# A hybrid decoder layer on one Trainium2 core: squares summed in small tiles, memory's norm later, quarters prepared over six units, pooling ahead of the local attention, constants loaded later

## The chip, the core and the metric

The kernel runs on one core of a Trainium2 chip. The core has a matrix engine (TensorE, PE in the profile), a vector engine (VectorE, DVE), a scalar engine (ScalarE, ACT) and a general one (GpSimd, POOL); SyncE (SP) here only issues loads. Each engine works through its own list of instructions in order and waits on semaphores for the others. The metric is the device time of one execution in microseconds (us); lower is better.

## The reference

One layer over 256 tokens of width 2048, in float32: a norm, one wide projection, four branches, a gated merge, an output projection.

```
h = rms_norm(x, g_pre[l])
proj = h @ w_in[l]
(a_val, a_gate, sq, sk, sv, s_gate, cq, ck, cv, c_gate, c_lr,
 mq, m_gate, g_logits) = jnp.split(proj, split_at, axis=-1)
y_a = pool_mixer(a_val, a_gate, w_pool[l], pool_scale[l])
y_b = swa_mixer(sq, sk, sv, s_gate)
y_c = gla_mixer(cq, ck, cv, c_lr, c_gate, w_alpha[l], b_alpha[l], g_gla[l])
y_m = mem_attn(mq, m_gate, mem, g_mem[l], w_mem_kv[l])
gates = jax.nn.sigmoid(g_logits.reshape(B, S, N_BRANCH, D_MODEL) + b_merge[l])
merged = (gates[:, :, 0] * (y_a @ w_br_pool[l]) + gates[:, :, 1] * (y_b @ w_br_swa[l])
          + gates[:, :, 2] * (y_c @ w_br_gla[l]) + gates[:, :, 3] * (y_m @ w_br_mem[l]))
x = x + rms_norm(merged @ w_out[l], g_post[l])
```

`pool_mixer` takes causal means over windows of 2, 4, 8 and 16 tokens, `swa_mixer` is an attention over local, dilated windows (12 heads), `gla_mixer` a gated linear attention in chunks of 64 tokens, `mem_attn` an attention into 256 memory tokens, whose keys and values come from `rms_norm(mem, g_mem) @ w_mem_kv`.

## The kernel before

**Products.** Every product of float32 matrices is made of three products in a shorter format: each operand is split into a high and a low part, and high x high, high x low and low x high are added up. The weights are split as they arrive: `split_w` (L135 to L141) has ACT copy the raw tile into a `hi` tile and DVE subtract that from the raw tile into a `lo` tile. There are five `hi` and five `lo` tiles. In the profile a split is an ACT instruction of L139 and a DVE instruction of L140, and the names say whose: `ck00h` is the high part of the first half of weight unit `ck0`. A `b_unit` projects 128 output features for all tokens: one load of 1 MB, two halves with a split each, 32 matmuls, and an evacuation of the result from PSUM by `two_sums` (ACT L203, then DVE L205 or L207). An `a_block` makes 512 columns for all tokens, in units of four k-tiles. 

**Staging.** The first stage runs over four chunks of memory's keys and values (`mem_chunk`, the names `mr`, `mhl`, `vm`, `km`), and within it the norm of x is prepared (`x_prep`, `xn`, `xsq`, the normalised halves `xhl`). The projections of the gated linear attention follow (`cq`, `ck`, `cv`, `cg`), then those of the memory attention (`mq`, `mg`), the values, queries, keys and gate of the local attention (`sv`, `sq`, `sk`, `sg`), and the pooling's (`av`, `ag`). Then four branch projections for each of four column blocks (`bmem`, `bswa`, `bgla`, `bpool`) are merged with their gates, and the output projection (`o0` to `o4`) ends the program.

**Two streams are woven into the units.** `queue` holds generators of small work (norms, attention heads, pooling). `pull(1)` runs one step of the first of them, twice in each unit or block unit; `drain(name)` runs steps until those of that name are done. `gate_stream` makes the merge gates' 8192 columns of logits, from ck0 on, as much as 1.13 of the units' work at a time; its results go to memory and come back as the tiles `g` in the branch stage. One part of this stream uses products of sums of weight blocks with differences of x's four quarters: `quarter_prep` makes these differences (`qs`, then their high and low parts `quarter`), eight steps, and `bias_prep` the rows of bias that the gates start from.

**Order of the instructions.** The program is written as above, and a scheduler that ranks by program order and by when buffers and engines come free lays out each engine's list, so a change in the program moves instructions on every engine. The buffers come in pools with a fixed number each: 13 of 8 KB a partition (`e8`: raw weights, `xhl`, `quarter`, the branch inputs y), 9 of 4 KB (`c4`), 7 of 2 KB (`c2`), two `sm`, two `acc` and four `seven` in PSUM. An instruction that writes into a buffer waits until its last user is done.

**What the change touches.** `squares` (L240) squares a chunk on ACT and adds it on DVE into a wide tile with two halves, `fold` (L247) folds that, and `inv_rms` (L251) sums over partitions on PE, takes the power on POOL and spreads the result into a row. `m_norm` (L273) does so for memory and scales `vm` (ACT L281) and `km`. `x_prep` starts with the first load of x. The constants (`walpha`, `big_cst`) are loaded on POOL's queue at the program's start (L500, L502). The queue holds km's evacuation, the bias, the quarters and memory's norm in this order; all quarters are drained after the four units cq, and the gates start there. The pooling projections stand behind the local attention's. `y_load` (L871) loads the branch inputs back, and `order` (L922) and `branches` set the order of the branch blocks.

## Time and profile before

| | |
|---|---|
| time, median of 3 runs | 1212.51 us (1210.67 to 1212.86) |
| the profiled execution's own time | 1207.7 us |
| its span, from the first to the last instruction | 1205.5 us |
| granted clock of PE over the span | 0.984 |
| DMA over the span | 301.84 MB, 250 GB/s |
| SP's queue of loads | 268.45 MB, 62.0% of the 16 DMA engines' time |
| POOL's queue | 22.81 MB, 5.4% |

The profile is one execution. A busy share says how long an engine had an instruction running; PE's durations overlap a little, and when the granted clock halves, a matmul of 512 columns takes 0.43 us in place of 0.23. What a change is worth is read from the stretches in which PE has nothing to run, and from what it waits for there.

### The profile page before, as it was taken

To read this page: it belongs to the slowest core of one execution; us is meant where nothing else is said; L and a number is where in the kernel's file an instruction comes from. 1 tells how busy PE (TensorE), PEld (TensorE's weight loads), DVE (VectorE), ACT (ScalarE), POOL (GpSimd) and SP (SyncE) were. 2 spreads that over 40 slices of the span, in tenths; PEclk is the share of its full clock that TensorE was granted. 3 is DMA by queue.
4 is the path that set the end of the run, shared out by engine and by line. 5 is a ranking of instruction groups with operands and counts; after the bars stand their busy time and mean duration, and the time that the engine had idled before them with its cause. 6 is when DMAs were issued, how large, how long until landed. Compare 5 with 4: busy or idle time off the path is not lost. (4 is left out here: it accounts for less than half of the span.)

```text
span 1205.5 us, 15389 instructions
## 1 busy us (share of the span) xinstructions
PE 1162.7 (96%) x5846; PEld 976.3 (81%) x5846; DVE 962.2 (80%) x1197; ACT 649.6 (54%) x823; POOL 55.3 (5%) x104
## 2 busy tenths in 40 slices
PE   8887999999999999999999999999999989999997
PEld 7765888878888878888888888888887868888787
DVE  6957878999899799789889968988997576776454
ACT  6635546575655655566566556556555444434341
POOL 0000000000101000000000000000001111110000
PEclk9988999999999999999999999999999989999999
DMA  9534658858877778688768767677769697749321
GB/s 359 226 140 161 235 202 310 304 206 290 289 263 253 273 273 303 227 290 288 248 255 282 241 231 272 242 280 270 261 255 357 243 366 263 249 177 384 106 70 71
DMA packets 79258, 301.84 MB, mean 250 GB/s; under 512 B 6176, under 2 KB 8608, under 8 KB 56784
## 3 DMA queue, kind: packets, MB, share of 16 engines
q1 hardware_dynamic: 65568, 268.45, 62.0%
q0 software_dynamic: 8288, 22.81, 5.4%
q10 hardware_dynamic: 5328, 9.60, 2.1%
q8 instruction: 46, 0.75, 0.2%
q14 instruction: 28, 0.23, 0.0%
HBM read 284.06 MB, written 16.78 MB: 250 GB/s over the span
## 5 line engine op out<-in xcount | busy, mean ns | idle before, releaser
L456 DVE TENSOR_TENSOR raw<-raw 128x1024 f32<-128x1024 f32 x64 | 78.0, 1220 | 11.0 <-DMA raw<-in_w_g 11.0
L462 DVE TENSOR_TENSOR raw<-raw 128x512 f32<-128x512 f32 x64 | 44.0, 689 | 1.2
L457 DVE TENSOR_TENSOR raw<-raw 128x512 f32<-128x512 f32 x64 | 43.7, 686 | 0.6
L898 POOL DMA_DIRECT2D g<-gd x32 | 17.2, 538 | 104.0 <-DVE merged L906 71.1
L906 DVE TENSOR_TENSOR merged<-merged,g 128x512 f32<-128x512 f32 x24 | 15.4, 684 | 0.0
L191 PE MATMUL ck0a<-xhl,ck00h 128*128 128x512 f32 x8 | 5.2, 648 | 8.0 <-ACT ck00h L139 8.0
L675 POOL DMA_DIRECT2D cgd<-cgate x4 | 2.2, 560 | 231.3 <-DVE cgate L220 231.3
L756 ACT ACTIVATE s<-s,st 128x384 f32<-128x384 f32 (+1 forms) x8 | 6.2, 774 | 11.8 <-DVE st L755 11.8
L780 POOL DMA_DIRECT2D ybd<-ybt x4 | 2.7, 682 | 177.6 <-DVE ybt L226 177.6
L953 DVE TENSOR_TENSOR yg<-o0a,gpost 128x512 f32<-128x512 f32 x2 | 1.4, 692 | 11.3 <-ACT oj L952 11.3
L191 PEld LDWEIGHTS ck0a<-xhl,ck00h 128*128 128x128 f32 x8 | 2.6, 325 | 8.9 <-ACT ck00h L139 8.3
L191 PE MATMUL cq3a<-xhl,cq30h 128*128 128x512 f32 x8 | 5.2, 645 | 4.8 <-ACT cq30h L139 4.8
L748 PE MATMUL sp<-k,q 128*128 128x128 f32 (+1 forms) x48 | 9.7, 331 | 0.0
L225 ACT ACTIVATE xhl<-xn 128x1024 fp32r<-128x1024 f32 x4 | 4.2, 1061 | 9.0 <-DVE xn L308 9.0
L748 PEld LDWEIGHTS sp<-k,q 128*128 128x128 f32 x48 | 7.2, 190 | 1.3 <-issue 0.6
L751 DVE SCALAR_TENSOR_TENSOR s<-big_cst,sp 128x128 f32<-128x128 f32 (+1 forms) x24 | 7.0, 347 | 1.5 <-PE sp L748 1.5
L424 ACT ACTIVATE c<-c 128x512 f32<-128x512 f32 x8 | 5.0, 628 | 5.5 <-DVE c L470 5.4
L919 ACT ACTIVATE mTh<-mtp 128x512 fp32r<-128x512 f32 x8 | 4.4, 596 | 6.4 <-PE mtp L917 6.4
L952 ACT ACTIVATE oj<-o0a 128x512 f32<-128x512 f32 x2 | 1.2, 597 | 11.9 <-PE o0a L147 11.9
L424 ACT ACTIVATE c<-p 128x512 f32<-128x512 f32 x8 | 4.7, 592 | 5.1 <-PE p L147 5.1
L191 PEld LDWEIGHTS cq3a<-xhl,cq30h 128*128 128x128 f32 x8 | 2.6, 326 | 5.8 <-ACT cq30h L139 5.3
L774 PE MATMUL po<-pt,sv 128*128 128x256 f32 x24 | 7.2, 380 | 0.0
(4605 smaller groups left out, 4611.5 us busy)
## 6 DMA issues: line engine op xcount, KB each, us to landing
raw<-in_w_g SPq DMA_DIRECT2D x112, 1024.0 KB, 5.4
raw<-in_w_sqk SPq DMA_DIRECT2D x24, 1024.0 KB, 5.0
raw<-in_w_sv SPq DMA_DIRECT2D x12, 1024.0 KB, 5.0
raw<-in_w_out SPq DMA_DIRECT2D x12, 1024.0 KB, 8.7
raw<-in_w_cqk SPq DMA_DIRECT2D x8, 1024.0 KB, 5.8
raw<-in_w_cg SPq DMA_DIRECT2D x8, 1024.0 KB, 5.5
raw<-in_w_av SPq DMA_DIRECT2D x8, 1024.0 KB, 6.2
raw<-in_w_ag SPq DMA_DIRECT2D x8, 1024.0 KB, 6.9
```

Source lines behind the costliest of these rows:

```text
L191: ten.matmul(a[:], lhsT=hi[:, ws], rhs=mov.both(k), start=(k == 0), stop=False)
L424: act.activation(dst, src, AF.Tanh, scale=0.5)
L456: vec.tensor_tensor(r4[:, :, 0, :], r4[:, :, 0, :], r4[:, 1, :, :], op=ALU.add)
L457: vec.tensor_tensor(r4[:, 1, 1, :], r4[:, 1, 1, :], r4[:, 0, 0, :], op=ALU.add)
L462: vec.tensor_tensor(r4[:, 0, 1, :], r4[:, 0, 1, :], r4[:, 1, 1, :], op=ALU.add)
L748: ten.matmul(parts[g], lhsT=q3[:, g, it * P : (it + 1) * P], rhs=k3[:, g, :nj], start=True, stop=True)
L751: vec.scalar_tensor_tensor(s[:, g, :], dist[:, g, :], SLOPES[g * 4 + hh], parts[g], op0=ALU.mult, op1=ALU.add)
L756: act.activation(s[:], s[:], AF.Exp, bias=st[:, 0:1], accum_out=st[:, 1:2])
L774: ten.matmul(po[:], lhsT=sv[g][:, 0, vs], rhs=pt[g][:, 0:T], start=(g == 0), stop=False)
L898: pool.dma_start(gs[t][:], gate_dram[b, j, t][:])
L906: vec.tensor_tensor(m, m, gs[t][:], op=ALU.add)
L919: act.activation(h, pp[:], AF.Copy, scale=0.5)
```

## The change

Six edits go together.

1. The squares of a chunk go into a tile of their own (x) or over the chunk itself (memory), and are added as two halves of 512 columns into a running total. The two remaining halves are added by PE, which makes two small matmuls for each half of the tokens in place of one. The column of inverse norms and the row spread from it are now two functions.
2. x's preparation begins one pull later. km and vm get their buffers when they are first written.
3. The column for memory is made behind km's evacuation; memory's norm itself is queued behind the cv blocks, and its scaling of vm waits for its place behind the split that ACT made last.
4. The quarters are drained, and the gates start, after six units (four cq, two ck) in place of four.
5. The two constants are loaded in `bias_prep`, behind a copy from x's inverse norms.
6. The pooling projections with their generators (`pool_group` and `mix`, word for word as they stood) move ahead of the local attention. All four pooling results now go through memory. The branch blocks come in the order memory, gated, pooling, local, and the local attention's inputs are loaded only before its first block.

```
-    def squares(sq, rawx, c):
-
+    def squares(total, dst, src, c):
+
+        act.activation(dst, src, AF.Square)
         if c == 0:
-            act.activation(sq[:, 0], rawx[:], AF.Square)
+            vec.tensor_tensor(total[:], dst[:, 0:2], dst[:, 2:4], op=ALU.add)
         else:
-            act.activation(sq[:, 1], rawx[:], AF.Square)
-            vec.tensor_tensor(sq[:, 0], sq[:, 0], sq[:, 1], op=ALU.add)
-
-    def fold(sq):
-        vec.tensor_tensor(sq[:, 0, 0:2], sq[:, 0, 0:2], sq[:, 0, 2:4], op=ALU.add)
-        vec.tensor_tensor(sq[:, 0, 0], sq[:, 0, 0], sq[:, 0, 1], op=ALU.add)
+            vec.tensor_tensor(dst[:, 0:2], dst[:, 0:2], dst[:, 2:4], op=ALU.add)
+            vec.tensor_tensor(total[:], total[:], dst[:, 0:2], op=ALU.add)
...
-    def inv_rms(name, sq, col, row):
+    def inv_rms_col(name, total, col):
 
         pc = sm(f"{name}pc", [P, 2, 2])
         for t in range(2):
-            ten.matmul(pc[:, t, :], lhsT=sq[:, 0, 0, t * P : (t + 1) * P], rhs=ones[:, 0:2], start=True, stop=True)
+            for i in range(2):
+                ten.matmul(pc[:, t, :], lhsT=total[:, i, t * P : (t + 1) * P], rhs=ones[:, 0:2],
+                           start=(i == 0), stop=(i == 1))
...
+    def inv_rms_row(name, col):
...
+        row = c2(f"{name}row", [P, T])
+        vec.tensor_copy(row[:], pr[:])
+        rows[name] = row
...
     def m_norm():
-        with tc.issue_after(cq0_split[1]):
-            fold(msq)
-        yield
-        yield from inv_rms("m", msq, mcol[:], mrow)
-        yield
-        for t in range(2):
-            act.activation(vm[:, t, :], vm[:, t, :], AF.Copy, scale=mcol[:, t : t + 1])
+        yield from inv_rms_row("m", mcol)
+        yield
+        km, vm = kv["k"], kv["v"]
+        with tc.issue_after(last_split[0]):
+            for t in range(2):
+                act.activation(vm[:, t, :], vm[:, t, :], AF.Copy, scale=mcol[:, t : t + 1])
...
     def x_prep():
+        yield
         for c in range(4):
             xn.append(c4(f"xn{c}", [P, 4, T]))
             sync.dma_start(xn[c][:], ins["xT"][:, 4 * c : 4 * c + 4, :])
-            squares(xsq, xn[c], c)
+            squares(xsq, c4(f"xs{c}", [P, 4, T])[:], xn[c][:], c)
...
     def km_evac():
+        km = kv["k"] = c4("km", [P, 4, T])
...
+        inv_rms_col("m", msq, mcol[:])
+        yield
...
     def bias_prep():
+        pool.tensor_copy(walpha[:, 0:1], xcol[0:16, 0:1])
+        pool.tensor_copy(big_cst[:, 0:1], xcol[:, 0:1])
+        pool.dma_start(walpha[:], ins["w_alpha"])
+        pool.dma_start(big_cst[:], ins["consts"])
         raw = c2("braw", [48, 512])
...
     queue.append(("quarters", quarter_prep()))
-    queue.append(("mnorm", m_norm()))
...
-    drain("quarters")
-    gate_stream[0] = all_gates()
     for h in range(4):
+        if h == 2:
+            drain("quarters")
+            gate_stream[0] = all_gates()
         b_unit(f"ck{h}", ins["w_cqk"][4 + h], h_at, plain_evac(gk[:, h, :]))
...
+    queue.append(("mnorm", m_norm()))
     queue.append(("gla", gla()))
...
-        if g < 2:
-            put_hilo(ya0[:, 0, fs, :], ya0[:, 1, fs, :], y[:])
-        else:
-            yt = c4(f"yat{g}", [P, 2, 2, T], R)
-            put_hilo(yt[:, 0], yt[:, 1], y[:])
-            pool.dma_start(ya_dram[0][:, :, fs, :], yt[:])
+        yt = c4(f"yat{g}", [P, 2, 2, T], R)
+        put_hilo(yt[:, 0], yt[:, 1], y[:])
+        pool.dma_start(ya_dram[g // 2][:, :, fs, :], yt[:])
...
-    drain("swa")
-    ym_at = y_load("ym", ym_dram)
-    yb_at = y_load("yb", yb_dram)
-    yc_at = y_load("yc", yc_dram)
-    drain("pool23")
-    ya1_at = y_load("ya", ya_dram)
...
+    for name in ("mnorm", "gla", "mem", "pool"):
+        drain(name)
+    at = {"mem": y_load("ym", ym_dram), "gla": y_load("yc", yc_dram), "pool": y_load("ya", ya_dram)}
+    branches = (("mem", 3, 1), ("gla", 2, 2), ("pool", 0, 2), ("swa", 1, 1))
...
-    order = [(0, 0), (0, 1), (1, 0), (1, 1), (0, 2), (0, 3), (1, 2), (1, 3)]
+    order = [(0, 0), (0, 1), (1, 0), (1, 1), (0, 2), (1, 2), (0, 3), (1, 3)]
...
+        if name not in at:
+            drain("swa")
+            at[name] = y_load("yb", yb_dram)
```

What this does to the engines' lists shows at three places. The first is ACT's list where the quarters are prepared, between the evacuation of unit cq2 and the splits of unit ck. Before:

```order
L203 ACTIVATE cq2s<-cq2a 128x256
L225 ACTIVATE quarter_539<-qs_709 128x512
L225 ACTIVATE quarter_540<-qs_710 128x512
L281 ACTIVATE vm<-vm,mcol 128x512 x2
L139 ACTIVATE cq30h<-raw_717 128x1024
L139 ACTIVATE cq31h<-raw_717 128x1024
L203 ACTIVATE cq3s<-cq3a 128x256
L225 ACTIVATE quarter_541<-qs_711 128x512
L225 ACTIVATE quarter_542<-qs_712 128x512
L225 ACTIVATE quarter_539<-qs_771 128x512
L225 ACTIVATE quarter_540<-qs_772 128x512
```

Two more such copies follow there, and then ck00h. In the changed kernel, from the same evacuation on:

```order
L203 ACTIVATE cq2s<-cq2a 128x256
L225 ACTIVATE quarter_551<-qs_754 128x512
L421 ACTIVATE brow<-braw 48x512
L203 ACTIVATE cq3s<-cq3a 128x256
L225 ACTIVATE quarter_552<-qs_755 128x512
L225 ACTIVATE quarter_553<-qs_756 128x512
L139 ACTIVATE ck00h<-raw_788 128x1024
L139 ACTIVATE ck01h<-raw_788 128x1024
L203 ACTIVATE ck0s<-ck0a 128x256
L225 ACTIVATE quarter_554<-qs_757 128x512
L225 ACTIVATE quarter_551<-qs_862 128x512
L139 ACTIVATE ck10h<-raw_840 128x1024
```

The splits cq30h and cq31h have moved ahead, behind km2s and before cq1s, the scaling of vm has left, and two copies stand ahead of each of the two ck units where six stood ahead of the first.

The second place is DVE's list where the first branch block is evacuated into `merged`, with the gate tile g. Before (win, pl, pt and plh are the last pooling group's):

```order
L903 SCALAR_TENSOR_TENSOR merged_8370<-g_8371,bmem0a_8375 128x512
L903 SCALAR_TENSOR_TENSOR merged_8370<-g_8373,bmem0a_8376 128x512
L808 TENSOR_TENSOR win_8457<-u_8123 128x2x256
L812 SCALAR_TENSOR_TENSOR pl_8475<-win_8457,u_8123 128x512
L816 TENSOR_TENSOR pt_8477<-win_8457,big_cst 128x1
L816 TENSOR_TENSOR pt_8480<-win_8457,big_cst 128x1
L817 TENSOR_TENSOR pl_8475<-pt_8477,u_8123 128x1
L817 TENSOR_TENSOR pl_8475<-pt_8480,u_8123 128x1
L226 TENSOR_TENSOR plh_8483<-pl_8475,plh_8483 128x512
L140 TENSOR_TENSOR bswa000l<-raw_8437,bswa000h 128x1024
```

In the changed kernel (st, s and sp are the softmax and the scores of the last head of the local attention):

```order
L140 TENSOR_TENSOR bgla011l<-raw_8492,bgla011h 128x1024
L897 SCALAR_TENSOR_TENSOR merged_8387<-g_8388,bmem0a_8392 128x512
L897 SCALAR_TENSOR_TENSOR merged_8387<-g_8390,bmem0a_8393 128x512
L837 RECIPROCAL st_8436<-st_8436 128x1
L140 TENSOR_TENSOR bmem100l<-raw_8542,bmem100h 128x1024
L838 TENSOR_SCALAR s_8412<-s_8412,st_8436 128x384
L140 TENSOR_TENSOR bmem101l<-raw_8542,bmem101h 128x1024
L830 SCALAR_TENSOR_TENSOR s_8483<-big_cst,sp_8484 128x256 x2
L830 SCALAR_TENSOR_TENSOR s_8483<-big_cst,sp_8485 128x256
L140 TENSOR_TENSOR bgla100l<-raw_8596,bgla100h 128x1024
L834 TENSOR_REDUCE st_8510<-s_8483 128x1
```

The pooling has left this place, the splits of the whole second block stand ahead of the evacuation, and the last head's softmax stands behind it, among the splits of the third and fourth block.

The third is POOL's list at the start of the branches (y.d, gd and in_w_pool are in memory; wpr is a pooling weight). Before:

```order
L874 DMA ym_8360<-ymd 128x2048
L874 DMA yb_8362<-ybd 128x2048
L874 DMA yc_8364<-ycd_555 128x2048
L874 DMA yc_8365<-ycd_556 128x2048
L856 MEMSET u_8123 128x2x16
L807 MEMSET win_8239 128x2x16
L851 DMA yad<-yat_8210 256x1x512
L825 DMA wpr_8237<-in_w_pool 128x512
L874 DMA ya_8368<-yad 128x2048
L898 DMA g_8371<-gd_3708 128x512
```

In the changed kernel:

```order
L880 DMA ym_8377<-ymd 128x2048
L880 DMA yc_8379<-ycd_565 128x2048
L880 DMA yc_8380<-ycd_566 128x2048
L880 DMA ya_8383<-yad_3352 128x2048
L880 DMA ya_8384<-yad_3353 128x2048
L859 DMA ybd<-ybt_8277 256x1x256
L892 DMA g_8388<-gd_3839 128x512
L892 DMA g_8390<-gd_4572 128x512
```

The first gate tile stands behind five loads of y and a store; the load of yb has moved behind the gate tiles of the pooling blocks.

More of the change, by code (lines that the diff above doesn't have):

```diff
@@ L682, in mem_head @@
     def mem_head(h):
+        km, vm = kv["k"], kv["v"]
         p0 = sm(f"mp{h}", [P, 2, T])
@@ L719, with pool_group @@
         queue.append(("mem", mem_head(h)))
+    PAD = 16
+    ya_dram = [spill(f"yad{i}", [P, 2, 4, T], R) for i in range(2)]
+    agate = {}
+    pooled = {}
+    u_tiles = {}
+    def pool_group(g):
+        w = POOL_WINDOWS[g]
+        u = u_tiles[g]
+        cur, sh = u, 1
+        while sh < w:
+            nxt = c4(f"win{g}{sh}", [P, 2, PAD + T])
+            if 2 * sh < w:
+                pool.memset(nxt[:, :, 0:PAD], 0.0)
+            vec.tensor_tensor(nxt[:, :, PAD:], cur[:, :, PAD:], cur[:, :, PAD - sh : PAD + T - sh], op=ALU.add)
+            cur, sh = nxt, 2 * sh
+            yield
+        res = c2(f"pl{g}", [P, 2, T])
+        vec.scalar_tensor_tensor(res[:], cur[:, :, PAD:], 1.0 / w, u[:, :, PAD:], op0=ALU.mult, op1=ALU.subtract)
+        n = w - 1
+        for ct in range(2):
+            tmp = tiny(f"pt{g}{ct}", [P, 16])
+            vec.tensor_tensor(tmp[:, :n], cur[:, ct, PAD : PAD + n], invc[:, g, :n], op=ALU.mult)
+            vec.tensor_tensor(res[:, ct, :n], tmp[:, :n], u[:, ct, PAD : PAD + n], op=ALU.subtract)
+        hl = c4(f"plh{g}", [P, 2, 2, T], R)
+        put_hilo(hl[:, 0], hl[:, 1], res[:])
+        pooled[g] = hl
+        yield
@@ L722 @@
+    for g in (3, 2, 1, 0):
+        u = c4(f"u{g}", [P, 2, PAD + T])
+        pool.memset(u[:, :, 0:PAD], 0.0)
+        u_tiles[g] = u
+        for ct in range(2):
+            b_unit(f"av{g}{ct}", ins["w_av"][2 * g + ct], h_at, plain_evac(u[:, ct, PAD:]))
+        agate[g] = c2(f"agate{g}", [P, 2, T])
+        for ct in range(2):
+            b_unit(f"ag{g}{ct}", ins["w_ag"][2 * g + ct], h_at, silu2_evac(agate[g][:, ct, :]))
+        queue.append(("pool", mix(g)))
     sv = [c4(f"sv{g}", [P, 2, 512]) for g in range(3)]
```

128 lines of the change are left out of this document (38 added, 90 removed).

## The prediction

> **What bounds the kernel now.** I read the page first, for the engines' shares.
>
> ```profile
> span 1205.5 us, 15389 instructions
> PE 1162.7 (96%) x5846; PEld 976.3 (81%) x5846; DVE 962.2 (80%) x1197; ACT 649.6 (54%) x823; POOL 55.3 (5%) x104
> ```
>
> TensorE (PE) is the bound: it idles 1205.5 - 1162.7 = 42.8 us in all, and its work hardly changes. So I ask only where those 42.8 us lie, and which of them the change can reach. The table of busy time by stretches comes next; its columns are the stretch, its length, then busy us of PE, PE's weight loads, DVE, ACT and POOL, the granted clock, the DMA share and GB/s.
>
> ```profile
> 0.00:60.00 60.00, 53.09 (x251) 42.82 (x251) 46.05 (x70) 39.10 (x53) 4.99 (x15) 0.97 0.77 294
> 78.00:108.00 30.00, 16.23 (x57) 12.54 (x58) 18.62 (x26) 14.24 (x20) 2.25 (x3) 0.72 0.20 69
> 108.00:900.00 792.00, 787.93 (x4025) 663.80 (x4024) 692.36 (x840) 464.09 (x588) 23.19 (x37) 1.00 0.75 263
> 900.00:930.00 30.00, 27.13 (x138) 22.63 (x137) 23.31 (x33) 15.98 (x21) 3.58 (x8) 0.94 0.96 371
> 964.00:980.00 16.00, 11.65 (x40) 8.65 (x39) 12.24 (x20) 6.93 (x9) 2.69 (x5) 0.79 1.01 410
> 980.00:1120.00 140.00, 140.00 (x640) 115.99 (x639) 97.11 (x113) 56.46 (x58) 13.50 (x27) 1.00 0.73 272
> 1120.00:1136.00 16.00, 13.75 (x52) 10.56 (x52) 8.36 (x8) 7.16 (x10) 0.00 (x0) 0.89 0.23 65
> ```
>
> PE is idle 6.9 us in the first 60, 13.8 in 78 to 108, 4.1 in the long middle, 2.9 before 930, 4.35 in 964 to 980 and 2.25 near 1130; the rest is the tail. The idle stretches cost a second time, because the granted clock falls with them. The same view for narrow stretches:
>
> ```profile
> 57.00:61.00 4.00, 1.12 (x5) 0.58 (x4) 2.88 (x4) 3.89 (x5) 0.00 (x0) 1.00 0.00 0
> 83.40:88.80 5.40, 4.93 (x14) 3.84 (x15) 2.95 (x3) 0.91 (x1) 0.00 (x0) 0.50 0.36 120
> 100.40:106.30 5.90, 5.43 (x16) 4.25 (x16) 5.74 (x5) 3.73 (x4) 0.00 (x0) 0.50 0.22 53
> 922.60:926.00 3.40, 3.40 (x13) 2.80 (x12) 3.37 (x6) 0.00 (x0) 0.00 (x0) 0.56 1.06 424
> 970.00:977.00 7.00, 5.72 (x13) 4.09 (x14) 5.93 (x6) 4.66 (x6) 1.08 (x2) 0.52 1.02 410
> ```
>
> At clock 0.50, half of the busy time is lost: 4.93 x 0.50 = 2.5 us and 5.43 x 0.50 = 2.7 us after the two long waits, 3.40 x 0.44 = 1.5 and 5.72 x 0.48 = 2.7 near the end. So 78 to 108 costs 13.8 + 2.5 + 2.7 = **19.0 us**, and the two stretches near the end cost 2.9 + 1.5 + 4.35 + 2.7 = **11.5 us**. Last, PE's waits by releaser:
>
> ```profile
> PE ck0a L191 <- ACT ck00h L139: 8.0, 1, 8.0
> PE cq3a L191 <- ACT cq30h L139: 4.8, 1, 4.8
> PE bswa0a L145 <- ACT bswa000h L139: 4.3, 1, 4.3
> ```
>
> In each, PE waits for a weight split that ACT makes late.
>
> **The change, part by part. Quarters over six units, memory's norm later.** Rows of the timeline of ACT, then of DVE (start, length, engine, line, what; in brackets the idle time before and its releaser):
>
> ```profile
> 71.98 0.39 ACT L203 ACTIVATE cq1s<-cq1a 128x256 f32<-128x256 f32 x1 [4.71 <-PE cq1a L192]
> 77.63 0.39 ACT L203 ACTIVATE cq2s<-cq2a 128x256 f32<-128x256 f32 x1 [4.48 <-PE cq2a L192]
> 81.08 1.33 ACT L281 ACTIVATE vm<-vm,mcol 128x512 f32<-128x512 f32 x2 [1.34 <-POOL mcol L257]
> 82.32 1.04 ACT L139 ACTIVATE cq30h<-raw 128x1024 fp32r<-128x1024 f32 x1
> 92.47 0.38 ACT L203 ACTIVATE cq3s<-cq3a 128x256 f32<-128x256 f32 x1 [8.17 <-PE cq3a L192]
> 92.76 0.62 ACT L225 ACTIVATE quarter<-qs 128x512 fp32r<-128x512 f32 x1
> 93.95 0.63 ACT L225 ACTIVATE quarter<-qs 128x512 fp32r<-128x512 f32 x1 [0.57 <-DVE qs L388]
> 99.30 1.04 ACT L139 ACTIVATE ck00h<-raw 128x1024 fp32r<-128x1024 f32 x1
> ...
> 92.89 0.42 DVE L207 SCALAR_TENSOR_TENSOR gq<-cq3a,cq3s 128x256 f32<-128x256 f32 x1 [6.54 <-ACT cq3s L203]
> 93.23 0.68 DVE L388 TENSOR_TENSOR qs<-xn,qs 128x512 f32<-128x512 f32 x1
> 100.38 1.22 DVE L140 TENSOR_TENSOR ck00l<-raw,ck00h 128x1024 fp32r<-128x1024 f32 x1 [0.26 <-ACT ck00h L139]
> ```
>
> The order of ACT before has two quarter copies and the scaling of vm, which waits for POOL's power, between the evacuation cq2s and the split cq30h. In the new order cq30h and cq31h stand before cq1s, so the 4.8 us wait of cq3 goes altogether. Between cq3s and ck00h there were six copies, 1.19 us apart (92.76 to 93.95, ACT and DVE taking turns); now there are two. But ACT still takes cq3s first, which cannot start before PE has ended cq3. So a wait stays: from cq3's end at 92.4, cq3s and the two copies put ck00h at 92.76 + 1.19 + 0.54 = 94.5 and its end at 95.5, 3.1 us after cq3; ck00l holds the second matmul 0.9 us more, and two bias matmuls fill some 0.6. That is 3.4 us idle. **The same wait now stands once more** between ck0 and ck1, where ck0s and two copies, the second behind DVE's gk and qs, precede ck10h: 3.1 + 0.8 = 3.9 us. Behind ck1 the next splits are already made (ck20h and gu0000h stand before ck1s). Idle after: 7.3 us. The clock fell after every idle stretch of over 4 us and not after 57 to 61, where PE was idle for 2.9 of 4 us; I take 2.0 us for each gap. So the stage costs 7.3 + 4.0 = 11.3 in place of 19.0: **gain 7.7 us**. Bounds: 1 (a third gap and full clock losses) to 14 (no clock loss, gaps half as long). Units are 5.65 us apart (71.98 to 77.63) and DVE was busy for 18.6 of 30 us here, so the moved copies have cover. The norm itself is used only by the memory heads, hundreds of us later; it is hidden in the units that follow cv, and without that cover it would cost its 1.33 us of ACT.
>
> **Start: small tiles for the squares, constants later.** From the view of the tile xsq, the DMA issues and ACT's timeline:
>
> ```profile
> L245 DVE TENSOR_TENSOR xsq<-xsq x3: 1222/1226/1227, 24.1 to 28.8; 128x1024 f32<-128x1024 f32 x3
> L248 DVE TENSOR_TENSOR xsq<-xsq x1: 687/687/687, 33.8 to 33.8; 128x512 f32<-128x512 f32 x1
>   ACT xsq L244: 2.3, 2
> ...
> big_cst<-in_consts POOLq DMA_DIRECT2D x1, 672.0 KB, 8.3
> ...
> 8.72 0.63 ACT L139 ACTIVATE vm01h<-raw 128x512 fp32r<-128x512 f32 x1 [1.17 <-DMA raw<-in_w_vm]
> ```
>
> Before, every square of x goes through one half of one tile, so ACT's square and DVE's addition take turns: DVE stands 2.3 us, in a stretch from which it then hardly rests until cq0. With a tile for each chunk these 2.3 us go. DVE's work grows: two additions of 0.69 us for one of 1.23 (twice three chunks, some 0.1 us each), and the first addition of memory comes on top, while x's fold goes: 0.8 us more. The constants take 0.69 MB from a saturated start; at 410 GB/s that is 1.7 us, and PE waits there for loads (vm01h). I count 1.0, since x now arrives interleaved with memory's weights, its last chunk later. Gain 2.3 - 0.8 + 1.0 = **2.5 us**; bounds 0 and 4.5. Four more two-column matmuls are under 0.9 us even at the mean of a full one (140.0/640 = 0.22). POOL's queue now holds constants, power, then the bias loads; brow on ACT stands behind cq2s, some 15 us after their issue; were it late, all of ACT behind it, cq3s and ck00h first, would be.
>
> **Pooling ahead of the local attention; branch order.** Rows of the chain, DVE, ACT, PE and the DMA issues:
>
> ```profile
> 960.55 6.58 DMA g<-gd
> ...
> 966.40 1.51 DVE L903 SCALAR_TENSOR_TENSOR merged<-g,bmem0a 128x512 f32<-128x512 f32 x2
> ...
> 969.61 0.63 ACT L225 ACTIVATE plh<-pl 128x512 fp32r<-128x512 f32 x1 [3.85 <-DVE pl L817]
> 970.15 1.04 ACT L139 ACTIVATE bswa000h<-raw 128x1024 fp32r<-128x1024 f32 x1
> ...
> 920.55 0.50 PE L191 MATMUL ag11a<-xhl,ag110h 128*128 128x512 f32 x1 [1.03 <-ACT ag110h L139]
> ...
> ym<-ymd POOLq DMA_DIRECT2D x1, 1024.0 KB, 12.8
> ```
>
> Before, DVE waits for the gate tile g, then makes the last pooling windows, ACT copies plh, and only then bswa000h: 4.35 us of PE. Afterwards no pooling is left there, and bgla0's eleven us of matmuls (48 x 0.22) follow bmem0 with their splits made. What is late next: five loads of y (1 MB each) and five weight tiles, all wanted within 30 us after the last gate matmul. 10.5 MB at 410 GB/s are 25.6 us, and g stands behind the y loads on POOL's queue. PE ends bgla0 at 2.8 + 2 x 5.65 + 5.3 + 10.5 = 30 us, counted from that matmul (half a unit, two units, 24 and 48 matmuls). DVE, held by merged<-g until about 26, has still 8 us to do (the evacuation, four splits of 1.13, the scores of head 3) before the transposes that PE meets 2.7 us into bmem1: about 1.5 us of wait, up to 5 if g lands at 29. Where the gates end, sq32 meets the shortage of split buffers that held ag11, once (1.1 us) where before it was twice. With 1.4 us for the transposes' copies between PE's pieces and 2.0 for the clock, I take 1.1 + 1.5 + 1.4 + 2.0 = 6.0 us for 11.5: **gain 5.5 us**, bounds 1 and 9.5. The last head's output has 28 us of PE work (half of bgla1, 96 matmuls of pooling) for a store and a load, 11.4 us at most by the row of yad below and 12.8 by that of ym. The middle loses nothing and gains nothing: the same DVE work in another order, at 692 of 792 us, and two more stores of 0.5 MB at a DMA share of 0.75. Bounds: 4.1 us, all that is idle there, and -5.
>
> **Sum.** 7.7 + 2.5 + 5.5 = 15.7 us. The profiled execution took 1207.7 us (span 1205.5 and 2.2 around it), so it would take 1192.0. It is 4.8 below the median of the runs, 1212.5; from the median, **1196.8 us**.
>
> **Rivals.**
> (1) A third gap, behind ck1, and 2.7 us of clock at each: 7.3 + 3.5 + 8.1 = 18.9 of 19.0 remain; 1204.4. For it speaks that ACT is in order and the last three copies stand ahead of ck21h; against it that half of ck2 and 24 gate matmuls have their splits.
> (2) g lands late. In the rows ym took 12.8 us for what 410 GB/s move in 2.6. If weights and y's share the engines evenly, POOL's 6 MB take 6/0.205 = 29 us, DVE ends 3.5 us later, and 1200.3 comes out. The Trainium skill's page "DMA: Bandwidth & Descriptors", section "Queues, rings and completion order", says that a DMA engine takes turns between the queues it has work for; the row of ym agrees with that, and my 25.6 us assume that the weights run dry early.
> (3) The gaps are too short for the clock: as in 57 to 61, it stays at 1.00 through gaps of 3.4 and 3.9 us. Then 4.0 us less: 1192.8. The page "TensorE: Matmul & The Clock Gate", section "HAM oscillation — how this bites in real kernels", of the Trainium skill asks that gaps stay under some 3.4 us, one window of its monitor, so that the clock holds; the fall at 922.6, after a wait of 1.03 us and a shorter one, speaks against so sharp a rule.
> (4) The stalls only move (PE in order, another split late at each place) or the start stays bound by its loads: 1211, no change.
> (5) Slower: the wide buffers run out. Pooling's four u tiles now live beside km, vm, mq, mgate and the gated attention's tiles in nine buffers, and a u takes the one that a stored yct leaves. DVE, in order, then waits for a store:
>
> ```profile
> DMA to landing us min/median/max: 5.1/5.4/11.4
> ```
>
> That is the row of the tile yad, a store of the same size. Splits made ahead cover one unit, 5.65 us. A landing of 11.4 costs 5.75 us and 1.7 of clock, four times 30 us: 1227. It decides where a store lands over 5.65 us after DVE's turn; the median of 5.4 speaks against it.
>
> **How the numbers follow.** Forecast 0.50 (by its terms' likely errors 1191 to 1203), rival 1 0.12, rival 2 0.12, rival 3 0.10, rival 4 0.08, rival 5 0.08. Faster by over 0.2%, which is about what a measurement of this kernel can tell from no change: 0.50 + 0.12 + 0.12 + 0.10 = 0.84; within it 0.08; slower 0.08. From 1189 to 1207 the range takes in the forecast and rivals 1 to 3 and leaves out 4 and 5 and the outermost of the bounds.
>
> **What would show it.** PE waiting for cq30h should be gone, and ck0a and ck1a should wait 2.5 to 4 us each for ck00h and ck10h, the clock below 1 behind at least one. cq0's first matmul should start near 56.7 in place of 59.2. bswa0 should wait for nothing; a wait of 1 to 5 us should stand at bmem1 or the transposes tp. I am wrong if waits of DVE for DMA appear at u, if the middle idles over 9 us, or if ck2 waits as ck0 does.

## The result, and the profile after

The changed kernel takes 1191.59 us (median of 4 runs, 1190.69 to 1192.68) against 1211.59 us before (1207.81 to 1212.86): a ratio of 0.984, with a 95% interval of 0.9816 to 0.9865. The forecast was 1196.8. The profiled execution spans 1188.5 us where that of before spans 1205.5. From the page:

```profile
span 1188.5 us, 15408 instructions
PE 1157.8 (97%) x5854; PEld 974.5 (82%) x5854; DVE 960.9 (81%) x1201; ACT 646.2 (54%) x823; POOL 59.3 (5%) x109
```

PE idles 1188.5 - 1157.8 = 30.7 us, 12.1 less than before. It is also busy 4.9 us less for the same matmuls: that is clock. Both together are the 17.0 us of the spans. The stretches tell where, first the changed kernel (stretch, length, busy us of PE, weight loads, DVE, ACT and POOL, granted clock, DMA share, GB/s):

```profile
0.00:78.00 78.00, 73.65 (x365) 61.49 (x366) 59.82 (x96) 47.75 (x67) 7.92 (x20) 0.98 0.77 294
78.00:108.00 30.00, 23.04 (x101) 18.52 (x100) 16.32 (x22) 11.41 (x17) 0.00 (x0) 0.83 0.30 102
108.00:880.00 772.00, 763.69 (x3900) 643.35 (x3899) 684.12 (x840) 456.76 (x579) 27.87 (x44) 1.00 0.75 266
880.00:980.00 100.00, 99.47 (x514) 84.07 (x513) 74.86 (x99) 50.71 (x69) 7.68 (x14) 1.00 0.84 316
```

Then the kernel before, for the stretches that the prediction had not cut in this way:

```profile
0.00:78.00 78.00, 70.48 (x351) 58.00 (x352) 56.99 (x88) 45.81 (x65) 4.99 (x15) 0.98 0.70 267
...
108.00:880.00 772.00, 767.93 (x3920) 646.78 (x3919) 673.62 (x815) 453.50 (x574) 23.19 (x37) 1.00 0.75 264
880.00:980.00 100.00, 92.78 (x472) 77.75 (x471) 75.12 (x110) 49.01 (x66) 10.21 (x20) 0.95 0.80 305
```

| PE idle, us | before | after | forecast of the change |
|---|---|---|---|
| 0 to 78 | 7.5 | 4.3 | 2.5 less |
| 78 to 108 | 13.8 | 7.0 | 13.8 to 7.3 |
| 108 to 880 | 4.1 | **8.3** | none |
| 880 to 980 | 7.2 | **0.5** | 7.2 to 4.0 |
| rest | 10.2 | 10.5 | none |

Two rows came as forecast. Two did not: the branches' start became nearly free, and the middle lost 4.2 us. The waits of PE by releaser (us in total, times, longest):

```profile
PE ck1a L191 <- ACT ck10h L139: 3.2, 1, 3.2
PE ck0a L191 <- ACT ck00h L139: 2.5, 1, 2.5
PE p L145 <- ACT p1c L457: 2.2, 3, 1.0
PE o1a L145 <- ACT o100h L139: 1.7, 1, 1.7
PE cq0a L192 <- DVE cq00l L140: 1.4, 1, 1.4
PE sp L827 <- DVE k L205: 1.3, 1, 1.3
```

The waits for cq30h, for bswa000h and at ag11 are gone. ck0 and ck1 wait as forecast; p behind p1c (a gate's first sum) and sp behind k are new, in the middle. ACT's timeline shows why ck0 and ck1 wait:

```profile
82.65 0.38 ACT L203 ACTIVATE cq3s<-cq3a 128x256 f32<-128x256 f32 x1 [4.29 <-PE cq3a L192]
82.93 0.62 ACT L225 ACTIVATE quarter<-qs 128x512 fp32r<-128x512 f32 x1
84.13 0.63 ACT L225 ACTIVATE quarter<-qs 128x512 fp32r<-128x512 f32 x1 [0.57 <-DVE qs L393]
84.66 1.04 ACT L139 ACTIVATE ck00h<-raw 128x1024 fp32r<-128x1024 f32 x1
...
95.19 0.38 ACT L203 ACTIVATE ck0s<-ck0a 128x256 f32<-128x256 f32 x1 [8.55 <-PE ck0a L192]
95.47 0.62 ACT L225 ACTIVATE quarter<-qs 128x512 fp32r<-128x512 f32 x1
96.67 0.63 ACT L225 ACTIVATE quarter<-qs 128x512 fp32r<-128x512 f32 x1 [0.57 <-DVE qs L393]
97.20 1.04 ACT L139 ACTIVATE ck10h<-raw 128x1024 fp32r<-128x1024 f32 x1
```

ACT stands idle for 4.29 and 8.55 us, then does the evacuation and two copies, and only then the split that PE stands still for. The clock, in narrow stretches of the same table:

```profile
58.00:62.00 4.00, 3.50 (x12) 3.08 (x13) 4.00 (x5) 2.64 (x3) 1.73 (x4) 0.57 0.36 76
86.00:92.50 6.50, 6.03 (x19) 4.75 (x20) 2.69 (x3) 0.65 (x1) 0.00 (x0) 0.51 0.47 161
99.50:103.00 3.50, 3.44 (x12) 3.01 (x13) 3.50 (x4) 2.53 (x3) 0.00 (x0) 0.55 0.36 77
```

Behind the two waits it loses 6.03 x 0.49 + 3.44 x 0.45 = 4.5 us, where 4.0 was forecast.

### The profile page after: what moved, and what is told of

Its sections match the earlier page's. It is cut to its first block, busy times and chain, and to the rows that moved or that the text cites. A ratio compares the mean times of both kernels' runs of the same rounds, so it can differ in the third digit from the quotient of the medians.

```text
span 1188.5 us, 15408 instructions
## 1 busy us (share of the span) xinstructions
PE 1157.8 (97%) x5854; PEld 974.5 (82%) x5854; DVE 960.9 (81%) x1201; ACT 646.2 (54%) x823; POOL 59.3 (5%) x109
## 4 chain that ended last, share of the span: by engine, by line
PE 73%; DVE 6%; DMA 3%; ACT 2%; issue 2%; DVEq 0%; ACTq 0%; POOLq 0%; POOL 0%
PE q L145 5%; PE q L146 5%; PE q L147 5%; DMA raw<-in_w_g 2%; PE p L145 1%; PE p L146 1%; PE p L147 1%; DMA raw<-in_w_cg 1%; PE o1a L146 1%; PE sv2a L146 1%; PE sv0a L145 1%; DMA gd<-c 1%; PE sv0a L147 1%; PE sv0a L146 1%; PE sv2a L145 1%
## 5 line engine op out<-in xcount | busy, mean ns | idle before, releaser
L468 DVE TENSOR_TENSOR raw<-raw 128x1024 f32<-128x1024 f32 x64 | 77.9, 1218 | 10.2 <-DMA raw<-in_w_g 10.1
L827 PE MATMUL sp<-k,q 128*128 128x128 f32 (+1 forms) x48 | 10.2, 335 | 1.3 <-DVE k L205 1.3
L948 DVE TENSOR_TENSOR yg<-o0a,gpost 128x512 f32<-128x512 f32 x2 | 1.4, 692 | 11.3 <-ACT oj L947 11.3
L641 POOL TENSOR_TENSOR ms<-ms,half 128x2 f32<-128x2 f32 x4 | 5.7, 1430 | 35.1 <-DVE ms L640 35.1
L191 PE MATMUL ck1a<-xhl,ck10h 128*128 128x512 f32 x8 | 4.2, 533 | 3.2 <-ACT ck10h L139 3.2
L629 POOL TENSOR_TENSOR sq<-sq 128x256 f32<-128x256 f32 x4 | 4.6, 1156 | 52.6 <-ACT sq L628 45.0
L337 DVE SCALAR_TENSOR_TENSOR mhl<-mr,vecs,mhl 128x256 fp32r<-128x256 f32 x16 | 6.8, 479 | 0.5 <-issue 0.3
## 6 DMA issues: line engine op xcount, KB each, us to landing
raw<-in_w_cqk SPq DMA_DIRECT2D x8, 1024.0 KB, 11.3
```

What stands on the lines that cost most here:

```text
L191: ten.matmul(a[:], lhsT=hi[:, ws], rhs=mov.both(k), start=(k == 0), stop=False)
L468: vec.tensor_tensor(r4[:, :, 0, :], r4[:, :, 0, :], r4[:, 1, :, :], op=ALU.add)
L827: ten.matmul(parts[g], lhsT=q3[:, g, it * P : (it + 1) * P], rhs=k3[:, g, :nj], start=True, stop=True)
```

## The experiments

Each ran against the kernel before on the same chip. The chip was not the same for all runs, so two of them are compared most safely by their ratios.

| run | median us | ratio to before (95%) |
|---|---|---|
| changed kernel | 1191.6 | 0.984 (0.9816 to 0.9865) |
| quarters_over_four | 1203.8 | 0.9937 (0.9918 to 0.9955) |
| quarters_four_gates_six | 1189.9 | 0.9832 (0.9811 to 0.9853) |
| quarters_norm_alone | 1232.5 | 1.0193 (1.0171 to 1.0215) |
| splits_ahead | 1180.0 | 0.9745 (0.9727 to 0.9763) |
| both_ahead | 1178.1 | 0.9735 (0.9711 to 0.9758) |
| pooling_back | 1205.0 | 0.9953 (0.994 to 0.9967) |
| pooling_alone | 1210.9 | 0.9998 (0.998 to 1.0016) |
| y_loads_late | 1204.4 | 0.9949 (0.9933 to 0.9964) |
| swa_second | 1213.8 | 1.003 (1.0017 to 1.0043) |
| constants_early | 1193.1 | 0.9858 (0.9837 to 0.9879) |
| squares_one_tile | 1193.1 | 0.9857 (0.9834 to 0.9879) |
| gate_share_lower | 1190.4 | 0.983 (0.9808 to 0.9852) |

**Is it the spreading of the quarters that gains?** First it is undone in the changed kernel.

```diff
     for h in range(4):
-        if h == 2:
+        if h == 0:
             drain("quarters")
             gate_stream[0] = all_gates()
```

> The changed kernel with the quarters drained ahead of ck0 again, as before the change; all else as changed. Theory of the forecast (spreading the quarters is what saves time here): most of the 7.7 us come back, about 1199 us against 1191.6. Rival (spreading only divides the same copies): seven copies stand between cq3s and ck00h, so one wait of about 9 us at ck0 and one clock loss of some 2.7 us take the place of two waits (7.0 us idle together) and two losses (2.9 and 1.6): 11.7 against 11.5, so 1190.5 to 1193 us; the gain of this stage then came from cq30h standing ahead of the copies and of vm's scaling.

It came out 12 us slower, more than either theory gave. The wait of PE, then the table by stretches:

```profile
PE ck0a L191 <- ACT ck00h L139: 8.6, 1, 8.6
```

```profile
78.00:108.00 30.00, 20.97 (x95) 16.95 (x94) 22.63 (x30) 17.22 (x24) 0.00 (x0) 0.83 0.36 136
108.00:880.00 772.00, 755.96 (x3835) 636.09 (x3834) 672.52 (x825) 444.52 (x563) 26.55 (x43) 1.00 0.74 260
```

The stage behaves as the rival said: one wait of 8.6 us, 9.0 us idle in place of 7.0. The largest part of the loss is elsewhere, in the middle: 16.0 us idle in place of 8.3. The edit moves a second thing, which the prediction had not priced: the stream of gates, whose matmuls and splits fill up the units, begins two units earlier and meets other units from there on. The next run parts the two.

```diff
     for h in range(4):
-        if h == 2:
+        if h == 0:
             drain("quarters")
+        if h == 2:
             gate_stream[0] = all_gates()
```

> The changed kernel with the quarters drained ahead of ck0, but the stream of gates still starting at ck2. It parts the two things that quarters_over_four moved. Theory (what cost it 10 of its 12 us was the gates, which began two units earlier and so fell beside other units): the wait at ck0 is 8.6 us again with a low clock behind it, the middle (108 to 880) idles 8 to 9 us as in the changed kernel, 1192 to 1195 us. Rival (copies made at once, seven in a row, delay DVE and ACT for long after): the middle idles 14 us or more, 1200 us or more.

Stretches of this kernel:

```profile
78.00:108.00 30.00, 20.97 (x108) 17.43 (x107) 21.38 (x28) 14.32 (x21) 0.00 (x0) 0.83 0.29 105
108.00:880.00 772.00, 763.04 (x3892) 643.66 (x3891) 678.53 (x831) 456.23 (x575) 27.74 (x44) 1.00 0.75 265
```

The theory holds: the stage idles the same 9.0 us as in the run before, the middle is back at 9.0, and the time, 1189.9, cannot be told from the changed kernel's. **Spreading the quarters by itself gains nothing that the time shows; where the gates start is worth 13 to 14 us (1203.8 against 1189.9; ratios 0.9937 against 0.9832).** By the spans of the two profiled executions it is 16.4 us: 8.8 of PE's idle time, 7.0 of them in the middle, and 7.6 of PE's busy time for the same matmuls, which is clock. Then the new drain and the later place in the queue were made alone, on the kernel before.

```diff
-    queue.append(("mnorm", m_norm()))
...
-    drain("quarters")
-    gate_stream[0] = all_gates()
     for h in range(4):
+        if h == 2:
+            drain("quarters")
+            gate_stream[0] = all_gates()
...
+    queue.append(("mnorm", m_norm()))
     queue.append(("gla", gla()))
```

> The kernel before with one part of the change alone: quarters drained and gates started ahead of ck2, memory's norm queued behind cv. Its squares, constants and pooling are those of before. Forecast's assignment (this part takes 7.7 us and cq3's wait with it): no wait at cq3, 1203 to 1205 us. Rival (cq3's wait goes with the edits of the start, which change what ACT has ready when cq3's weights are split; here the copies and vm's scaling still stand ahead of cq30h): cq3 waits 4 to 5 us as before, ck0's wait falls from 8.0 to about 3, none arises at ck1, 1205 to 1208 us if the middle keeps its 4 us of idle time.

Neither time was near: 1232.5. The waits of PE, then the row of memory's squares (msq) in the view of that tile, then DVE's waits from 130 to 300:

```profile
PE cq3a L191 <- ACT cq30h L139: 4.8, 1, 4.8
...
PE ck0a L191 <- ACT ck00h L139: 3.2, 1, 3.2
```

```profile
L284 DVE TENSOR_TENSOR km<-km,msq x4: 418/424/424, 247.6 to 254.4; 128x256 f32<-128x256 f32 x4
```

```profile
DVE raw L456 <- DMA raw<-in_w_g: 11.3, 5, 3.6
```

In the stage the rival is right: cq3 still waits 4.8 us and ck0 3.2. Drain and queue place do not take cq3's wait away: vm's scaling still runs at 82.5 us (the view of the tile vm), ahead of cq30h, although the program now has it behind cv; the line that orders it behind the last split (in the new m_norm) is not in this kernel. The middle idles 772 - 752.0 = 20.0 us, and the gates' weights come late there: before, the same two rows read

```profile
L284 DVE TENSOR_TENSOR km<-km,msq x4: 418/418/419, 127.5 to 128.5; 128x256 f32<-128x256 f32 x4
```

```profile
DVE raw L456 <- DMA raw<-in_w_g: 0.9, 3, 0.4
```

In the kernel before, msq is one of the 13 wide buffers that also hold the weights. With the norm moved behind cv it stays taken until 254 us instead of 128. That this is what delays the loads fits both rows, but it was not tried apart. In the changed kernel msq is a small tile, and its norm at 222 to 229 us costs nothing that shows.

**What do the two waits at ck0 and ck1 still hold?** Here the splits are ordered ahead of the evacuations (on ACT and DVE).

```diff
+    def evac_behind(split, evac):
+        def run(name, a):
+            with tc.issue_after(split[0]), tc.issue_after(split[1]):
+                evac(name, a)
+        return run
...
+    ck = {0: b_split("ck0", ins["w_cqk"][4])}
+    b_unit("cq3", ins["w_cqk"][3], h_at, evac_behind(tuple(last_split), plain_evac(gq[:, 3, :], SCALE)))
     for h in range(4):
...
+        if h < 2:
+            ck[h + 1] = b_split(f"ck{h + 1}", ins["w_cqk"][5 + h])
+            evac = evac_behind(tuple(last_split), evac)
+        b_unit(f"ck{h}", ins["w_cqk"][4 + h], h_at, evac, ck.get(h))
```

> The changed kernel, with the weight splits of ck0, ck1 and ck2 ordered ahead of the evacuations of cq3, ck0 and ck1 on ACT and DVE. If the order on ACT is all that is waited for: the waits at ck0a and ck1a go with their 7.0 us of idle time and 4.5 us of clock, so 1179 to 1182 us. Rival (five split buffers, or the copies, hold something else up): the waits move to cq3, ck2 or ck3, and the time stays within 1187 to 1193 us.

```profile
78.00:108.00 30.00, 29.31 (x155) 24.34 (x154) 24.67 (x33) 18.45 (x26) 0.00 (x0) 1.00 0.45 162
```

That is the stage of this kernel: 0.7 us idle, clock 1.00. 1180.0 us is 11.6 below the changed kernel, where 7.0 + 4.5 had been counted. The weights and the buffers were there; only the order on ACT and DVE stood in the way. The same edit at the next such place:

```diff
+        if j == 0:
+            pre = b_split("o10", ins["w_out"][1, 0])
+            with tc.issue_after(last_split[0]), tc.issue_after(last_split[1]):
+                done()
```

> splits_ahead, and o1's first two weight splits ordered ahead of o0's evacuation on ACT and DVE. If these splits have their weights and buffers by then: o1a's wait of 1.7 and 0.5 us goes, 1177 to 1178.5 us. Rival (the splits wait for a buffer that o0 frees at its end): 1179.5 to 1181 us.

The wait at o1a is gone: PE is busy for the whole 145 us from 980 to 1125, where it was for 142.75. The median is 1178.1, 1.9 lower; the intervals overlap, so the trace carries this one. It is the lowest median here.

**What did the pooling's move gain?** Undone in the changed kernel (its place, the branch order, the loads of y):

```diff
-    for g in (3, 2, 1, 0):
...
     for j in range(3):
         a_block(f"sv{j}", [ins["w_sv"][j, u] for u in range(4)], h_at, 512, sv_evac(j))()
...
+    for g in (3, 2, 1, 0):
...
     gates(1e9)
...
-    branches = (("mem", 3, 1), ("gla", 2, 2), ("pool", 0, 2), ("swa", 1, 1))
+    branches = (("mem", 3, ym_at, 4),
+                ("swa", 1, yb_at, 4),
+                ("gla", 2, yc_at, 8), ("pool", 0, ya_at, 8))
```

> The changed kernel with pooling behind the local attention again, with the branch order and the loads of y of before; the rest as changed. Forecast's sizes: 5.5 us come back, 1197 us, the middle (108 to 880) idle as in the changed kernel, the branches' start costing 6 more. Rival from the trace of the changed kernel: the start of the branches costs about 11 us again where it cost 0.5, and the middle's new 4 us of waits (p behind p1c, sp behind k) go, since they come from pooling's new place: 1198 us with 4 us idle in the middle. Third: those waits come from another part: 1202 us, with 8 us idle in the middle.

```profile
108.00:880.00 772.00, 766.47 (x3906) 647.26 (x3906) 673.10 (x820) 453.81 (x579) 22.59 (x37) 1.00 0.74 261
880.00:980.00 100.00, 90.53 (x448) 75.06 (x447) 76.79 (x110) 47.89 (x64) 10.77 (x21) 0.93 0.83 311
```

13.4 us come back, more than any of the three sums. 880 to 980 idles 9.5 us and loses 0.07 x 90.53 = 6.3 of clock, 15.8 in all; the middle idles 5.5, so by this pair of profiles 2.8 us of its 8.3 belong to pooling's new place. (Kernels whose middle is that of the changed kernel idle 6.7 to 9.1 us there, so 1 to 4 us is what can be said.) Then pooling's move alone, on the kernel before:

```diff
-    drain("mnorm")
-    drain("gla")
-    drain("mem")
-    drain("swa")
...
+    for name in ("mnorm", "gla", "mem", "pool"):
+        drain(name)
...
-    order = [(0, 0), (0, 1), (1, 0), (1, 1), (0, 2), (0, 3), (1, 2), (1, 3)]
+    order = [(0, 0), (0, 1), (1, 0), (1, 1), (0, 2), (1, 2), (0, 3), (1, 3)]
```

> The kernel before with the other part alone: pooling ahead of the local attention, the new branch order and loads of y; the gates still start at ck0. Forecast's additive sum: 5.5 us less, 1206 us, middle idle 4 us. Rival from quarters_over_four (pooling's place and the gates' start act together): the branches' start loses 0.5 to 1.5 in place of 11.5, but the middle (108 to 880) idles 11 to 16 us, 1207 to 1214 us.

```profile
108.00:880.00 772.00, 758.13 (x3853) 635.34 (x3852) 673.48 (x825) 447.84 (x567) 29.61 (x43) 1.00 0.75 264
880.00:980.00 100.00, 97.70 (x516) 83.23 (x515) 71.52 (x93) 50.51 (x69) 7.82 (x14) 0.98 0.83 307
```

The rival holds: the start of the branches gains 4.9 us of idle time and 2.7 of clock, the middle idles 13.9 us in place of 4.1, and nothing is left (0.9998). In these runs the move gains only together with the gates' later start.

**Why was the branches' start free, when a late g had been counted?** The changed kernel's timeline of POOL, and of ACT where the last gate is written:

```profile
913.35 0.55 POOL L880 DMA_DIRECT2D ym<-ymd  x1 [36.99 <-PE q L147]
...
922.67 0.53 POOL L880 DMA_DIRECT2D ya<-yad  x1 [4.44 <-DVE gv3131l L140]
...
941.38 1.22 POOL L892 DMA_DIRECT2D g<-gd  x2
...
934.57 0.60 ACT L436 ACTIVATE c<-q 128x512 f32<-128x512 f32 x1 [0.30 <-PE q L147]
```

The loads of y are issued from 913 to 923 us, 12 to 21 us before the last gate is written at 934.57; the first of them goes when PE's q is done, the last when a split of DVE is, and by these rows that is when their buffers come free. The loads of g are issued from 941.38 us on. The next kernel holds the loads of y until that gate is written, as the prediction had counted them.

```diff
+        last_gate[0] = c12
...
         for i in range(len(src)):
+            if name != "yb":
+                pool.tensor_copy(tiles[i][:, 0, 0, 0:1], last_gate[0][:, 0:1])
             pool.dma_start(tiles[i][:], src[i][:])
```

> The changed kernel; POOL issues its loads of ym, yc and ya only when the last gate tile is written (about 935 us), as the forecast counted them, and g behind them. Forecast's working: g then lands 26 to 29 us after the last gate matmul, DVE is held at merged, and PE waits 1.5 to 5 us at bmem1 or at the transposes, with about 2 us of clock: 1194 to 1198 us. Rival (the transfers have room even then): no wait over 0.5 us from 935 to 980, 1191 to 1192.5 us.

PE's waits, and the timeline of POOL and DVE:

```profile
PE bmem1a L145 <- DVE merged L901: 7.3, 1, 7.3
...
PE tp L847 <- DVE s L840: 2.0, 1, 2.0
...
PE bmem1a L146 <- DVE bmem100l L140: 1.3, 1, 1.3
```

```profile
942.18 1.09 POOL L896 DMA_DIRECT2D g<-gd  x2 [4.05 <-DMA gd<-c]
...
970.92 0.69 DVE L901 SCALAR_TENSOR_TENSOR merged<-g,bmem0a 128x512 f32<-128x512 f32 x1 [18.79 <-DMA g<-gd]
```

The place and the releaser are those of the forecast, the size is not: g lands 29 us after its issue and 40 us after the last gate (ACT's c<-q starts at 930.66 us there), DVE stands 18.8 us, PE 10.6, and the time is 12.8 us above the changed kernel. Last, the order of the branches alone is put back:

```diff
-    branches = (("mem", 3, 1), ("gla", 2, 2), ("pool", 0, 2), ("swa", 1, 1))
+    branches = (("mem", 3, 1), ("swa", 1, 1), ("gla", 2, 2), ("pool", 0, 2))
...
-    order = [(0, 0), (0, 1), (1, 0), (1, 1), (0, 2), (1, 2), (0, 3), (1, 3)]
+    order = [(0, 0), (0, 1), (1, 0), (1, 1), (0, 2), (0, 3), (1, 2), (1, 3)]
```

> The changed kernel with pooling ahead of the local attention, but the branches in the order of before (swa second). Theory (the order is as needed as the place: head 3's scores, transposes, store and load must now end within bmem0): PE waits 12 to 20 us between bmem0 and bswa0, with a low clock behind it, 1206 to 1214 us. Rival (pooling's place alone empties the branches' start): waits of at most 5 us there, 1192 to 1197 us.

```profile
PE bswa0a L145 <- DMA yb<-ybd: 14.7, 1, 14.7
```

PE stands for the load of the last head's output, and the time, 1213.8, lies 0.3% above that of before. With all the edits but the order the kernel would have become slower.

**The start, edit by edit.**

```diff
-        pool.dma_start(walpha[:], ins["w_alpha"])
-        pool.dma_start(big_cst[:], ins["consts"])
...
     big_cst = cst.tile([P, 1344], F32, name="big_cst")
+    pool.dma_start(walpha[:], ins["w_alpha"])
+    pool.dma_start(big_cst[:], ins["consts"])
```

> The changed kernel with the two loads of constants (0.7 MB) issued at the start again. Forecast's term: 1.0 of the transfer's 1.7 us shows, cq0 starts that much later, 1192.6 to 1193.3 us. Rival (the loads of the start are not what PE waits for, or they wait in a queue of their own): cq0 starts as in the changed kernel, 1191.0 to 1192.2 us.

```diff
+        xs = c4("xs", [P, 4, T])
         for c in range(4):
...
-            squares(xsq, c4(f"xs{c}", [P, 4, T])[:], xn[c][:], c)
+            squares(xsq, xs[:], xn[c][:], c)
```

> The changed kernel with one tile for the squares of all four chunks of x, so that ACT's square waits for DVE's additions of the chunk before. Forecast's term: 2.3 us of DVE's time in turns with ACT come back, cq0 starts 1.5 to 2.5 us later, 1193 to 1194 us. Rival (DVE has other work to take in these turns, the order of instructions adapts): cq0 starts within 0.5 us of the changed kernel, 1191 to 1192.2 us.

Both medians are 1.5 us above the changed kernel's, within the intervals, so the first matmul of cq0 has to decide. PE's timeline of the kernel before, of the changed one, of constants_early, of squares_one_tile, and last of gate_share_lower (further down), whose start is not edited:

```profile
59.16 0.50 PE L191 MATMUL cq0a<-xhl,cq00h 128*128 128x512 f32 x1 [1.93 <-ACT cq00h L139]
```

```profile
56.64 0.49 PE L191 MATMUL cq0a<-xhl,cq00h 128*128 128x512 f32 x1 [0.66 <-ACT cq00h L139]
```

```profile
58.34 0.50 PE L191 MATMUL cq0a<-xhl,cq00h 128*128 128x512 f32 x1 [0.68 <-ACT cq00h L139]
```

```profile
58.84 0.58 PE L191 MATMUL cq0a<-xhl,cq00h 128*128 128x512 f32 x1 [2.14 <-ACT cq00h L139]
```

```profile
58.52 0.50 PE L191 MATMUL cq0a<-xhl,cq00h 128*128 128x512 f32 x1 [0.67 <-ACT cq00h L139]
```

By these rows the constants cost 1.70 us and the shared tile 2.20. But gate_share_lower begins as late with the start of the changed kernel, and so does both_ahead, at 58.93; the six other kernels of the table with that start begin cq0 between 56.33 and 56.77 us. In the two late ones ACT waits 0.8 and 1.0 us for PE at the split vm31h, which waits for nothing in the changed kernel. Both ran on another chip than the six, and on that chip kernels with the start of before (quarters_norm_alone, pooling_alone) begin cq0 at 59.07 and 59.33 us. One late start therefore does not price an edit; the trace has to show the way. For the constants it does: in constants_early ACT waits 1.7 us for the load behind vm01h, in the changed kernel it does not, and all that follows up to cq0 stays some 1.7 us later, as much as had been counted for their transfer. For the shared tile it does not: ACT begins the first xhl earlier than in the changed kernel (45.72 against 46.40 us), and the later ones fall behind while DVE splits km30 and km31 between x's chunks. Those 2.20 us come with another order of instructions; that ACT and DVE taking turns cost them is not shown.

**How far does the middle depend on the gates' place?**

```diff
-GATE_SHARE = 1.13
+GATE_SHARE = 1.11
```

> The changed kernel with the gates' share of each unit's time at 1.11 in place of 1.13: no other work, but the gates' pieces fall beside other units from the middle of cv on. Theory (the idle time of the middle is set by which unit a piece falls beside): it differs by over 2 us from the 8.3 of the changed kernel, either way, and the time with it (1185 to 1189 or 1194 to 1198 us). Rival (it is set by pooling's own work on ACT and DVE): 7.3 to 9.3 us idle, 1190.5 to 1193 us.

The middle idles 772 - 765.5 = 6.5 us, between the two bounds, and the time cannot be told from the changed kernel's. swa_second and y_loads_late, whose edits lie behind the middle, idle 7.0 and 6.7 us there, so 6.5 against 8.3 is hardly more than this spread. The run decides nothing; that the gates' place matters rests on quarters_over_four, quarters_four_gates_six and pooling_alone, and by what mechanism it does stays open.

## Why the prediction was right, and where its reasons were not

**Quarters and norm: the size right, the cause half wrong.** It forecast 11.3 us for 78 to 108 and measured 7.0 + 4.5 = 11.5. But it wrote that the quarters' spread and the norm's later place take cq3's wait away. quarters_norm_alone, which has both, keeps that wait at 4.8 us, and the two runs that drain the quarters at ck0 in the changed kernel have none at cq3. So another edit puts cq30h ahead of the copies, the order within m_norm or one of the start's. Two of the start's are ruled out: constants_early and squares_one_tile keep cq30h ahead of cq1s (69.39 against 74.23 us, and 69.34 against 74.18). The rest, m_norm, the smaller msq and xsq and the later buffers of km and vm, was not parted. And quarters_four_gates_six shows that the spreading cuts one wait in two that together are only 2 us shorter (7.0 us idle against 9.0). The prediction's own "the same wait now stands once more" had said nearly that.

**Start: right where it was measured, but not everywhere.** 2.5 us forecast, 59.16 - 56.64 = 2.52 measured, and cq0 at 56.7 forecast, 56.64 measured. But with the same start cq0 begins at 58.52 in gate_share_lower and 58.93 in both_ahead, against 59.07 and 59.33 with the start of before on that chip, so there the same edits gain 0.1 to 0.8 us; why is open. The term of the constants was undersized (1.0 for 1.70). The shared tile's 2.20 is near the 2.3 counted for the turns, but was not shown to come from them, so what DVE's added work takes (0.8 counted) stays open.

**Pooling ahead: the failing step is "what is late next".** It took 6.0 us for the stretch where 0.5 was measured, and a gain of 5.5 where 11 came (6.7 us of idle time and 0.05 x 92.78 = 4.6 of clock). It let the loads of y and g begin at the last gate matmul. The trace shows those of y 12 to 21 us before the last gate is written. On its own premise the price was too low as well: 12.8 us by y_loads_late. Rival (2), queues that share, fits what happens there: the Trainium skill's page "DMA: Bandwidth & Descriptors", section "Queues, rings and completion order", has a DMA engine take turns between its queues, and the 29 us of g behind 5 MB of y agree with that.

**Middle: the failing step is "loses nothing and gains nothing".** It idles 4.2 us more. The step weighed DVE's work, its new order and two stores; the largest new waits, PE's for ACT's p1c and DVE's k, are not in that account. By pooling_back 2.8 of the 8.3 us belong to pooling's new place (1 to 4, given the spread of the middle), the rest of the 4.2 to the other edits. Nor did it see that the quarters' drain, which moves the gates' start, decides the price: with the gates' start of before, pooling's place costs 9.8 us in the middle (13.9 - 4.1). The idle time stayed just under the 9 us that the prediction had named as a sign of being wrong.

**Sum.** 15.7 us were forecast and 17.0 measured between the two profiled executions; the medians differ by 20.0, since the profiled execution of before, at 1207.7, lies 3.9 below the median of its runs. The sum came near by luck: 5.8 us of gain at the branches' start that were not counted and 4.2 us of loss in the middle that were not counted either nearly cancel. It was also read as a sum of parts, which it is not: pooling alone gains nothing, quarters and norm alone lose 23 us, all but pooling (pooling_back) gains 0.5%, some 6 us, and all six together 20. Of the rivals, (1) did not occur, as ck2 does not wait; (3) falls, since the clock fell behind both gaps; (4), no change, lies outside the interval; of (5) the trace shows one wait of DVE for a store, 2.3 us at pl and none at u.

## What to carry to other kernels

Where filler work runs beside the main units, moving its start is an edit with a price of its own (here 13 to 14 us), and edits that gain nothing alone can gain together. Ask of a load not only what it stands behind in its queue, but when the buffer comes free that its issue waits for. Before a shift of 2 us in one profile is put down to an edit, look for the same shift in kernels without it. When an engine stands idle for microseconds just ahead of an evacuation and makes the next unit's split only behind it, order the split first: that took 11.6 us more off this kernel, with no work removed.

## What had not been expected of the hardware

The clock's answer to the same short waits differs from run to run. At cq0, PE waits 0.7 us and then 1.3 to 1.4 in the changed kernel, in y_loads_late and in both_ahead alike. The stretch behind it, of the changed kernel, of y_loads_late and of both_ahead (which reaches cq0 2.3 us later):

```profile
60.00:78.00 18.00, 18.00 (x99) 15.66 (x98) 10.11 (x17) 6.35 (x12) 2.61 (x5) 0.95 0.67 238
```

```profile
60.00:78.00 18.00, 18.00 (x105) 15.87 (x105) 11.68 (x19) 6.46 (x12) 2.34 (x5) 1.00 0.63 238
```

```profile
60.00:78.00 18.00, 17.22 (x82) 14.89 (x83) 12.25 (x15) 8.98 (x14) 2.81 (x6) 0.81 0.50 170
```

By the clock's column, the third from the end, it costs nothing in y_loads_late and 0.19 x 17.22 = 3.3 us in both_ahead; in the changed kernel the fall begins ahead of this stretch and costs 0.43 x 3.50 = 1.5 us from 58 to 62. The Trainium skill's page "TensorE: Matmul & The Clock Gate", section "HAM oscillation — how this bites in real kernels", asks only that gaps stay under some 3.4 us; here waits of 2.1 us together were followed by 0.57 (58 to 62 us of the changed kernel). The 2.2 us at o1a were followed by no fall at all in the changed kernel, and by 0.89 from 1120 to 1136 in the kernel before. Terms of up to 3 us for the clock can be forecast as a range, not as a number.
